# Output projection of a hybrid decoder step: tokens become the stationary operand, 512 weight columns stream past them

## The chip, the cores and the metric

One core of a Trainium2 chip runs the whole step in one launch. The metric is the device time of one execution in microseconds (us); a row of the profile gives times in us or, where it says so, in ns, counted from the first instruction of the profiled execution.

## What is computed

A decoder layer takes 512 prompt tokens and 8 x 4 sample tokens (544 in all, model width 2048) through an mLSTM branch and an attention branch. The change touches the last step alone: the merged branches `y`, times a 2048 x 2048 weight, plus a scaled residual, through a LayerNorm.

```python
def _layernorm(x, w, b):
    mu = jnp.mean(xf, axis=-1, keepdims=True)
    var = jnp.mean(jnp.square(xf - mu), axis=-1, keepdims=True)
    return (xf - mu) * lax.rsqrt(var + LN_EPS) * w + b
...
    y = (sigmoid(g_m) * einsum('btc,cd->btd', br_m, w_proj_m)
         + sigmoid(g_a) * einsum('btc,cd->btd', br_a, w_proj_a))
    out = jnp.einsum('btc,cd->btd', y, w_out)
    return _layernorm(DN_ALPHA * x + out, ln_w, ln_b)
```

All inputs and outputs are F32. Products keep F32 accuracy by a split: each operand is a rounded part (`wh`, `yh`, type F32R) and a rest (`wl`, `yl`), and three products `wh*yh`, `wh*yl`, `wl*yh` are summed in PSUM.

## The kernel before

The last stages are three runs over 16 tiles of 128 output columns each: the two branch projections (lines 1383 and 1399) and the output projection (line 1540). Each tile loads its weights from HBM as two halves of 8 k-tiles (`load_half`, line 182, the DMA of line 184 into one of three `raw` buffers of the pool `wr`), casts them on ScalarE (line 191, `wh`) and takes the rest on VectorE (line 192, `wl`), into two buffers of the pool `wp`; `products` (line 195, the matmul of line 200) then runs over k, the three products and two pieces of the token columns. The weights are stationary, the tokens move, and a result has its output column on the partition and its token along the bank.

The run at line 1399 makes `y`: VectorE multiplies the PSUM tile by a gate (line 1404), adds the other branch (line 1405), and `hilo` (lines 231 and 232) writes the parts `yh` and `yl`, 2048 x 544 each.

The output projection cuts the 544 tokens into 256 + 288 (`CUT`). Thirteen column tiles go through `gemm`; ScalarE copies the bank (`evac`, line 1463), TensorE transposes the copy back to tokens on partitions (line 1448 for the prompt, line 1455 for the 32 samples), and VectorE adds it to the residual `z` or `zs`, scaled by ALPHA (lines 1449, 1456). `zs` holds the samples as four quarters of 512 columns on four groups of 32 partitions. The last three column tiles multiply only the tokens from 256 on in that way. The other 256 tokens get those 384 columns from `rows_of` (line 1526, matmul of line 1536), in which the tokens are stationary and the weights move, while VectorE finishes the tiles that are complete: statistics (line 1461), `moments` (line 1474, with a power on GpSimd), and `finish` (line 1493), which takes 1280 columns in two passes on VectorE (lines 1505 and 1510) and 768 by VectorE, ScalarE and GpSimd (lines 1505, 1507, 1508), and stores.

The residual rows, the LayerNorm vectors and the samples' quarters of them come by DMAs of SyncE (`load_rows`, line 1423, `load_ln`, line 1431), in the same in-order queue as the weights. A scheduler sets the order of each engine's instructions; TensorE's is fixed by the code's own order only inside a `manual_schedule` block, which this stage does not use. PSUM has eight banks: four `sm` tiles (pool `psB`) and either two double-bank `mm` tiles or four `bank` tiles (`open_psum`, line 96).

Of the kernel before, what the change touches and what calls it, by code (L numbers as in the profile page):

```python
# [20 lines left out]
D = 2048  # L21
# [52 lines left out]
def _build(tc, nc, i, o, es):  # L74
# [1344 lines left out]
    wD = pool(esD, "wD", 1)  # L1419
# [8 lines left out]

    cq = d1.tile([128, 128], F32, name="cq")
# [10 lines left out]
    CUT = ((0, 0, 256), (1, 256, 288))  # L1440

    def add_residual(ct, ot, lo, hi):

        cs = slice(ct * 128, ct * 128 + 128)
        pt = sm()
        nb_ = min(hi, 4) - lo
        for t in range(lo, min(hi, 4)):
            PE.transpose(pt[:, (t - lo) * 128:(t - lo) * 128 + 128], ot[:, t * 128:t * 128 + 128], ident)  # L1448
        V.scalar_tensor_tensor(z[:, lo:lo + nb_, cs], z[:, lo:lo + nb_, cs], ALPHA, blk(pt[:, 0:nb_ * 128], nb_),
                               op0=ALU.mult, op1=ALU.add)  # L1450
        if hi == 5:
            q, c0 = ct // 4, (ct % 4) * 128
            r = slice(q * 32, q * 32 + 32)
            pt2 = sm()
            PE.transpose(pt2[:32, 0:128], ot[:, SEQ:T], ident)
            V.scalar_tensor_tensor(zs[r, c0:c0 + 128], zs[r, c0:c0 + 128], ALPHA, pt2[:32, 0:128],
                                   op0=ALU.mult, op1=ALU.add)

    def stats(lo, hi, c4):
        for t in range(lo, min(hi, 4)):  # L1460
            V.bn_stats(stt[:, t, c4], z[:, t, c4 * 512:c4 * 512 + 512])

    def evac(ot, ps, parts=(0, 1)):
        for f, c, w in CUT:
            if f in parts:
                A.copy(ot[:, c:c + w], ps[:, f, :w])

    def residual_task(ct, ot):
        add_residual(ct, ot, 0, 5)
        if ct % 4 == 3:  # L1470
            yield
            stats(0, 4, ct // 4)

    def moments(t):
        m = mv[:, t]
        if t < 4:
            V.bn_aggr(m[:, 0:2], stt[:, t])
            V.tensor_scalar(m[:, 1:2], m[:, 1:2], EPS, None, op0=ALU.add)
        else:
            V.bn_stats(stt[:, t, 0], zs)  # L1480
            V.bn_aggr(m[:, 0:2], stt[:, t, 0:1])
            V.scalar_tensor_tensor(m[:, 1:2], m[:, 0:1], m[:, 0:1], m[:, 1:2], op0=ALU.mult, op1=ALU.add)
            pm = sm()
            PE.matmul(pm[:, 0:2], cq[:], m[:, 0:2], start=True, stop=True)
            V.tensor_copy(m[:, 0:2], pm[:, 0:2])
            V.scalar_tensor_tensor(m[:, 3:4], m[:, 0:1], m[:, 0:1], m[:, 1:2], op0=ALU.mult, op1=ALU.subtract)
            V.tensor_scalar(m[:, 1:2], m[:, 3:4], -1.0, EPS, op0=ALU.mult, op1=ALU.add)
# [25 lines left out]
    def tail_task(ct, ot):  # L1513
        add_residual(ct, ot, 2, 5)
        yield

    def add_rows(t):

        cs = slice(D - G3 * 128, D)
        V.scalar_tensor_tensor(z[:, t, cs], z[:, t, cs], ALPHA, rows[t][:, 0:G3 * 128], op0=ALU.mult, op1=ALU.add)  # L1520
        stats(t, t + 1, 3)
        moments(t)

    rows = {}

    def rows_of(t, meanwhile):
        ps = rows[t] = sm()
        for k in range(KT):
            if k == 2:
                meanwhile()  # L1530
            yk = slice(t * 128, t * 128 + 128)
            hi, lo = yh_[k // 4][:, k % 4, yk], yl_[k // 4][:, k % 4, yk]
            for n, (a, p) in enumerate(((hi, 0), (hi, 1), (lo, 0))):
                for c, w, b in ((0, 256, w2[k // 8][p][:, k % 8].rearrange("p g c -> p (g c)")),
                                (256, 128, w1[k // 8][p][:, k % 8])):
                    PE.matmul(ps[:, c:c + w], a, b, start=(k == 0 and n == 0 and c == 0),
                              stop=(k == KT - 1 and n == 2 and c > 0), skip_group_check=True)

    G3 = 3
    for ct in range(16 - G3):  # L1540
        raws = [load_half(wo, ct * 128, half) for half in range(2)]
# [61 lines left out]
```

## Time and profile before

| | |
|---|---|
| median of 3 runs | 2565.08 us (2562.29 to 2566.04) |
| span of the profiled execution, first to last instruction | 2561.7 us |
| VectorE's last pass ends | 2557.7 us |
| TensorE's granted clock, mean over the span | 0.993 |
| ScalarE, GpSimd busy | 46%, 14% |
| instructions | 48818 |

The span is what the profile shows of one execution; the time of a run also holds what lies around it, and the profiled execution's own time is not given apart, so the median stands 3.4 us above this span and the fastest run 0.6. A row of an engine's timeline gives start, duration, engine, line, operation, output and input, shape and count, and in brackets how long the engine sat idle before it and what ended that. Matmuls overlap, so the distance between two starts, not the duration, tells what one costs.

### The profile page before, as it was taken

What the parts mean: (1) busy time and instruction counts of PE and PEld (TensorE: products, weight loads), DVE (VectorE), ACT (ScalarE), POOL (GpSimd) and SP (SyncE); (2) the same over time, 40 slices, a digit from 0 to 9 for tenths busy, and PEclk for the clock granted to TensorE, in tenths of its full rate; (3) what the DMA queues carried; (4) which work ended last, traced back from release to release, by engine and by line L of the source; (5) the groups of instructions that cost most, each with busy time, mean ns of one, the idle gap of its engine ahead of it and who ended that gap; (6) DMA issues with size and microseconds to landing.
All of it is one profiled execution on the core that took longest, in us unless ns stands there. A gap on an engine that the chain in (4) does not pass through costs nothing.

```text
span 2561.7 us, 48818 instructions
## 1 busy us (share of the span) xinstructions
PE 2524.2 (99%) x19994; PEld 2464.3 (96%) x19994; DVE 1707.2 (67%) x2508; ACT 1173.2 (46%) x1908; POOL 362.3 (14%) x334
## 2 busy tenths in 40 slices
PE   8999999999999999999999999999999999999997
PEld 8999999999999999899999998999999999999997
DVE  7867777777777777687777877777856553333236
ACT  4447667666666655333433433434633332222221
POOL 2111211211111111121121222221000000000002
PEclk9999999999999999999999999999999999999999
DMA  6566666666666663477576575676655455446332
GB/s 196 139 160 157 151 156 154 152 158 148 157 160 146 156 161 89 119 230 235 154 236 212 168 227 163 185 235 207 187 171 172 162 179 155 139 135 189 106 97 86
DMA packets 537103, 421.86 MB, mean 165 GB/s; under 512 B 43536, under 2 KB 449344, under 8 KB 536592
## 3 DMA queue, kind: packets, MB, share of 16 engines
q1 hardware_dynamic: 526800, 382.04, 49.8%
q0 software_dynamic: 10080, 36.70, 7.9%
q8 instruction: 157, 2.57, 0.4%
q14 instruction: 66, 0.54, 0.1%
HBM read 297.66 MB, written 86.42 MB: 150 GB/s over the span
## 4 chain that ended last, share of the span: by engine, by line
PE 57%; DVE 1%; issue 0%; POOL 0%; ACT 0%; DVEq 0%
PE mm L200 21%; PE bank L597 17%; PE bank L599 9%; PE sm L1266 2%; PE sm L1085 1%; PE sm L1079 1%; PE sm L1298 1%; PE sm L1311 1%; PE sm L200 1%; DVE z L1505 0%; PE sm L1245 0%; PE sm L1321 0%; PE sm L1253 0%; DVE z L1510 0%; PE sm L1448 0%
## 5 line engine op out<-in xcount | busy, mean ns | idle before, releaser
L191 ACT CAST wh<-raw 128x1024 fp32r<-128x1024 f32 x604 | 632.8, 1048 | 978.5 <-PE bank L597 599.3
L192 DVE TENSOR_TENSOR wl<-raw,wh 128x1024 fp32r<-128x1024 f32 x604 | 750.1, 1243 | 367.3 <-ACT wh L191 359.9
L597 PE MATMUL bank<-xk,wh 128*128 128x272 f32 x2304 | 312.7, 288 | 1.3 <-DVE ev L622 1.3
L597 PEld LDWEIGHTS bank<-xk,wh 128*128 128x128 f32 x2304 | 297.7, 188 | 4.2 <-ACT wh L191 2.4
L577 DVE TENSOR_TENSOR raw<-raw,raw 128x1024 f32<-128x1024 f32 x218 | 276.5, 1270 | 5.5 <-DMA raw<-in_w_in 2.9
L200 PE MATMUL mm<-bh,wl 128*128 128x272 f32 x1024 | 214.0, 289 | 0.0
L200 PE MATMUL mm<-bh,wh 128*128 128x272 f32 x1024 | 213.6, 290 | 0.0
L200 PE MATMUL mm<-bl,wh 128*128 128x272 f32 x1024 | 213.3, 288 | 0.0
L599 PE MATMUL bank<-xk,wl 128*128 128x272 f32 x1152 | 168.1, 288 | 0.0
L616 POOL TENSOR_TENSOR ev<-p,ev 128x272 f32<-128x272 f32 x72 | 105.0, 1458 | 424.9 <-ACT ev L615 404.4
L200 PEld LDWEIGHTS mm<-bh,wh 128*128 128x128 f32 x1024 | 160.7, 188 | 2.3 <-issue 2.3
L200 PEld LDWEIGHTS mm<-bl,wh 128*128 128x128 f32 x1024 | 161.4, 188 | 0.0
L200 PEld LDWEIGHTS mm<-bh,wl 128*128 128x128 f32 x1024 | 160.9, 189 | 0.0
L599 PEld LDWEIGHTS bank<-xk,wl 128*128 128x128 f32 x1152 | 153.4, 189 | 0.0
L597 PE MATMUL bank<-n2h,wh 128*128 128x272 f32 x576 | 149.1, 290 | 1.9 <-ACT wh L191 1.9
L597 PE MATMUL bank<-s1h,wh 128*128 128x272 f32 x576 | 150.5, 292 | 0.0
L597 PE MATMUL bank<-s1l,wh 128*128 128x272 f32 x576 | 149.3, 292 | 0.0
L597 PE MATMUL bank<-s4h,wh 128*128 128x272 f32 x576 | 149.0, 290 | 0.0
L597 PE MATMUL bank<-a11h,wh 128*128 128x272 f32 x576 | 148.7, 290 | 0.0
L597 PE MATMUL bank<-n2l,wh 128*128 128x272 f32 x576 | 148.7, 291 | 0.0
L597 PE MATMUL bank<-a11l,wh 128*128 128x272 f32 x576 | 148.5, 291 | 0.0
L597 PE MATMUL bank<-n3l,wh 128*128 128x272 f32 x576 | 148.2, 290 | 0.0
(427 smaller groups left out, 5489.7 us busy)
## 6 DMA issues: line engine op xcount, KB each, us to landing
raw<-in_w_in SPq DMA_DIRECT2D x296, 512.0 KB, 4.4
raw<-raw POOLq DMA_DIRECT2D x70, 512.0 KB, 4.9
C<-in_state_mlstm_C SPq DMA_DIRECT2D x32, 1024.0 KB, 5.6
out<-C SPq DMA_DIRECT2D x64, 512.0 KB, 3.8
raw<-in_w_proj_a SPq DMA_DIRECT2D x32, 512.0 KB, 5.6
raw<-in_w_proj_m SPq DMA_DIRECT2D x32, 512.0 KB, 4.3
raw<-in_w_out SPq DMA_DIRECT2D x32, 512.0 KB, 4.3
d_sgm<-ev SPq DMA_DIRECT2D x16, 272.0 KB, 3.9
```

What stands on the lines that cost most here:

```text
L191: A.copy(wh[:], raw[:])
L192: V.tensor_tensor(out=wl[:], in0=raw[:], in1=r32(wh[:]), op=ALU.subtract)
L200: PE.matmul(ps[:, f, :w], a[:, kk], b(k, c, w), start=(k == 0 and n == 0), stop=(k == 15 and n == 2))
L577: V.tensor_tensor(out=w[out][:], in0=w[a][:], in1=w[b][:], op=ALU.add)
L597: PE.matmul(ps, wh[:, k], x(p, k), start=(first and k == 0 and p == 0), stop=False, skip_group_check=True)
L599: PE.matmul(ps, wl[:, k], x(0, k), start=False, stop=(k == 7), skip_group_check=True)
L616: G.tensor_tensor(out=c22, in0=p1, in1=c11, op=ALU.subtract)
L1079: PE.matmul(pC[c * 32:c * 32 + 32, :], qz[:, c], ct[:, c], start=(b == 0), stop=(b == NB - 1), tile_position=(0, c * 32))
L1085: PE.matmul(pu[:], Ab[:, c * 128:c * 128 + 128], r["V4"][:], start=True, stop=True)
L1266: PE.matmul(pp[:, 0:258], a[:, b * 128:b * 128 + 128], b_[:, b, f], start=(b == 0 and n == 0), stop=(b == 3 and n == 2))
L1298: PE.matmul(pp[:, 0:n], x_[c][:, b * 128:b * 128 + 128], y_[c][:, b * 128:SEQ], start=(c == 0 and m == 0), stop=(c == 3 and m == 2))
L1311: PE.matmul(pp[:, 0:258], x_[:, off:off + 128], y_[:, b, f], start=(b == 0 and n == 0), stop=(b == j and n == 2))
```

## The change

`y` becomes the stationary operand for the whole projection. Four blocks of 512 output columns are computed; in each, four banks hold the four tiles of 128 prompt tokens (`ps`), one more the samples (`acc`). Weights come in chunks of two k-tiles by 512 columns (`wide`), eight to a block; six chunks have buffers for their parts (two in `wp`, four in `wD`), three for their raw form. A result already has its token on the partition, so VectorE adds the residual straight from the bank (`add_rows`). The 32 sample tokens are no longer columns of the matmuls above: a copy `ysf` in F32 is the stationary operand of 32-column matmuls on four column groups, one k-tile each, against the raw F32 weights (`samples_by`); one more matmul with a selection matrix sums the four groups (`add_samples`). TensorE's order is fixed by the code (`manual_schedule`). In blocks 0 to 2 the tiles share each pair of chunks; in block 3 they share the first four chunks, then the samples take the last four, then the tiles are completed one by one, each followed by its LayerNorm.

```diff
+    ysf = pool(es, "ysp", 1, side="left").tile([128, KT, NS], F32, name="ysf")
...
         hilo(sg[:], yh_[ct // 4][:, ct % 4], yl_[ct // 4][:, ct % 4])
+        A.copy(ysf[:, ct], sg[:, SEQ:T])
...
-    wD = pool(esD, "wD", 1)
+    wD = pool(esD, "wD", 4)
...
+    def wide(cb, j):
+        raw = wr.tile([128, 2, 512], F32, tag="raw", name=nm("raw"))
+        nc.sync.dma_start(raw[:], wo[:, 2 * j:2 * j + 2, cb * 512:cb * 512 + 512])
+        p = wp if j % 6 < 2 else wD
+        wh, wl = (p.tile([128, 2, 512], F32R, tag=t_, name=nm(t_)) for t_ in ("wh", "wl"))
+        hilo(raw[:], wh[:], wl[:])
+        return wh, wl, raw
+
+    def rows_by(ps, t, ks, chunks):
+        yk = slice(t * 128, t * 128 + 128)
+        for k in ks:
+            wh, wl = (w[:, k % 2] for w in chunks[k // 2][:2])
             hi, lo = yh_[k // 4][:, k % 4, yk], yl_[k // 4][:, k % 4, yk]
+            for n, (a, b) in enumerate(((hi, wh), (hi, wl), (lo, wh))):
+                PE.matmul(ps[:], a, b, start=(k == 0 and n == 0), stop=(k == KT - 1 and n == 2))
+
+    def samples_by(ps, ks, chunks):
+        for k in ks:
+            g = k % 4
+            PE.matmul(ps[g * 32:g * 32 + 32, :], ysf[:, k], chunks[k // 2][2][:, k % 2], start=(k < 4), stop=(k >= KT - 4),
+                      tile_position=(0, g * 32))
+
+    def add_rows(t, cb, ps):
+        cs = slice(cb * 512, cb * 512 + 512)
+        V.scalar_tensor_tensor(z[:, t, cs], z[:, t, cs], ALPHA, ps[:], op0=ALU.mult, op1=ALU.add)
+        V.bn_stats(stt[:, t, cb], z[:, t, cs])
+
+    def add_samples(cb, sq, ps):
+        q = slice(cb * 32, cb * 32 + 32)
+        PE.matmul(ps[q, :], cc[:, C_SEL:C_SEL + 32], sq[:], start=True, stop=True, tile_position=(0, cb * 32))
+        V.scalar_tensor_tensor(zs[q], zs[q], ALPHA, ps[q, :], op0=ALU.mult, op1=ALU.add)
...
+    with tc.manual_schedule(engines={PE.engine}):
+        open_psum(True)
+        for cb in range(4):
+            mine, other = (sm, bank) if cb % 2 == 0 else (bank, sm)
+            chunks = {}
+            if cb == 0:
+                chunks.update({j: wide(cb, j) for j in range(2)})
+                for q in range(4):
+                    load_rows(q)
+            ps = [mine() for _ in range(4)]
+            acc = other()
+            last = cb == 3
+            for j in range(0, 4 if last else 8, 2):
+                for jj in (j, j + 1):
+                    if jj not in chunks:
+                        chunks[jj] = wide(cb, jj)
+                samples_by(acc, range(2 * j, 2 * j + 4), chunks)
+                for ks in ((2 * j, 2 * j + 1), (2 * j + 2, 2 * j + 3)) if last or j < 6 else (range(12, 16),):
+                    for t in range(4):
+                        rows_by(ps[t], t, ks, chunks)
+                        if not last and j == 6:
+                            add_rows(t, cb, ps[t])
+            if cb == 1:
+                load_ln()
+            if not last:
+                sq = ev(512)
+                A.copy(sq[:], acc[:])
+                add_samples(cb, sq, other())
+        for j in (4, 6):
+            for jj in (j, j + 1):
+                chunks[jj] = wide(cb, jj)
+            samples_by(acc, range(2 * j, 2 * j + 4), chunks)
+        sq = ev(512)
+        A.copy(sq[:], acc[:])
+        for t in range(4):
+            rows_by(ps[t], t, range(8, 12), chunks)
...
+            rows_by(ps[t], t, range(12, 16), chunks)
+            add_rows(t, 3, ps[t])
+            moments(t)
+            scale_of(t)
+            finish(t, LAST if t == 3 else CHUNKS)
```

At the first dots of the last loop tile 0 runs `add_samples` and the samples' statistics, tile 1 their normalisation and stores. `finish` keeps its passes, chunk by chunk.

Three places show how the built order moves. The first is SyncE's queue at the start of the output projection. Before, `raw_27165` is the sixth weight load of the stage (the second half of column tile 2), and the eight quarter loads follow `lb`:

```order
L1432 DMA cq<-in_consts 128x128
L1433 DMA lw<-in_ln_w 128x2048
L184 DMA raw_27165<-in_w_out 128x8x128
L1434 DMA lb<-in_ln_b 128x2048
L1437 DMA zs_26920<-in_ln_w 32x512
```

Now, with `raw_27101` the sixth weight load (chunk 5 of block 0, k-tiles 10 and 11) and the pair of quarter loads standing four times:

```order
L1433 DMA cq<-in_consts 128x128
L1434 DMA lw<-in_ln_w 128x2048
L1435 DMA lb<-in_ln_b 128x2048
L1438 DMA zs_26940<-in_ln_w 32x512
L1439 DMA zs_26941<-in_ln_b 32x512
...
L1478 DMA raw_27101<-in_w_out 128x2x512
L1478 DMA raw_27159<-in_w_out 128x2x512
```

Five weight loads stand ahead of `z` in both; the sixth has moved behind `lb` and all quarters, and the vectors that the code asks for after block 1 stand in block 0.

The second place is TensorE's queue in block 3, where the tiles' first halves end and their second halves begin. `raw_27928`, `raw_27934`, `raw_27944` and `raw_27950` are chunks 4 to 7, `sm_27799` the samples' accumulator, `bank_27798` and `bank_27795` tiles 3 and 0:

```order
L1491 MATMUL bank_27798<-wh_27872,yl_25036 128x512
L1497 MATMUL sm_27799<-raw_27928,ysf 32x512 x2
L1497 MATMUL sm_27799<-raw_27934,ysf 32x512 x2
L1497 MATMUL sm_27799<-raw_27944,ysf 32x512 x2
L1497 MATMUL sm_27799<-raw_27950,ysf 32x512 x2
L1491 MATMUL bank_27795<-wh_27930,yh_25033 128x512
L1491 MATMUL bank_27795<-wl_27931,yh_25033 128x512
```

Nothing like it stood there before: the samples were columns of each tile's matmuls. All four raw chunks are now read in one run, and nothing else of TensorE's lies between.

The third place is VectorE's queue at the end. Before, where the prompt tiles `z` finish (`sm_28731` and `sm_28872` are the two banks of `rows_of`):

```order
L1510 SCALAR_TENSOR_TENSOR z<-z,mv,lb 128x1280
L1520 SCALAR_TENSOR_TENSOR z<-z,sm_28731 128x384
L1486 SCALAR_TENSOR_TENSOR mv<-mv 128x1
L1496 SCALAR_TENSOR_TENSOR zs_26919<-zs_26919,mv,zs_26920 128x512
L1461 BN_STATS stt<-z 128x6
```

Now, with `bank_27797` and `bank_27798` the banks of tiles 2 and 3:

```order
L1460 SCALAR_TENSOR_TENSOR z<-z,mv,lw 128x1280
L1505 SCALAR_TENSOR_TENSOR z<-z,bank_27797 128x512
L1465 SCALAR_TENSOR_TENSOR z<-z,mv,lb 128x1280
L1506 BN_STATS stt<-z 128x6
L1443 BN_AGGR mv<-stt 128x2
L1445 TENSOR_SCALAR mv<-mv 128x1
L1460 SCALAR_TENSOR_TENSOR z<-z,mv,lw 128x768
L1460 SCALAR_TENSOR_TENSOR z<-z,mv,lw 128x1280
L1505 SCALAR_TENSOR_TENSOR z<-z,bank_27798 128x512
```

The add and the statistics of each tile now stand between the passes of the tile ahead of it, for all four tiles; before, two tiles went through this end and two had been finished ahead.

## Rows read from the trace of the kernel before

**Rows 1.** The page, whole span: busy time of the engines and the chain that ended last

```profile
PE 2524.2 (99%) x19994; PEld 2464.3 (96%) x19994; DVE 1707.2 (67%) x2508; ACT 1173.2 (46%) x1908; POOL 362.3 (14%) x334
...
PE 57%; DVE 1%; issue 0%; POOL 0%; ACT 0%; DVEq 0%
```

**Rows 2.** Timeline of TensorE, start and end of the output projection

```profile
2341.96 0.41 PE L200 MATMUL mm<-yh,wh 128*128 128x256 f32 x2
2342.21 0.41 PE L200 MATMUL mm<-yl,wh 128*128 128x256 f32 x2
...
2547.09 0.22 PE L1536 MATMUL sm<-wh,yl 128*128 128x128 f32 x1
```

**Rows 3.** Timeline of TensorE in the sample phase, 1169 to 1176

```profile
1169.51 1.16 PE L599 MATMUL bank<-s4h,wl 128*128 128x272 f32 x8
1170.60 1.07 PE L1079 MATMUL sm<-C,qz 128*32 128x512 f32 x8
1171.59 0.72 PE L1085 MATMUL sm<-V,Ab 128*128 128x512 f32 x2
1172.15 2.17 PE L597 MATMUL bank<-xk,wh 128*128 128x272 f32 x16
1174.16 1.17 PE L599 MATMUL bank<-xk,wl 128*128 128x272 f32 x8
1175.16 0.62 PE L1085 MATMUL sm<-V,Ab 128*128 128x512 f32 x2
1175.62 0.29 PE L597 MATMUL bank<-a11h,wh 128*128 128x272 f32 x1
```

**Rows 4.** Timeline of VectorE where the output projection starts

```profile
2342.16 0.72 DVE L1404 TENSOR_TENSOR c<-mm,c 128x544 f32<-128x544 f32 x1 [3.91 <-PE mm L200]
...
2343.56 1.22 DVE L192 TENSOR_TENSOR wl<-raw,wh 128x1024 fp32r<-128x1024 f32 x1
```

**Rows 5.** Timeline of SyncE's queue, 2340 to 2380 (start and time of the issue)

```profile
2345.28 0.52 SPq L1426 DMA_DIRECT2D z<-in_x_prompt  x1
...
2356.43 5.51 SPq L1434 DMA_DIRECT2D lb<-in_ln_b  x1
...
2370.96 0.31 SPq L1438 DMA_DIRECT2D zs<-in_ln_b  x1
2371.37 7.14 SPq L184 DMA_DIRECT2D raw<-in_w_out  x4
```

**Rows 6.** Waits of SyncE's queue, 2340 to 2380: total, times, longest

```profile
SPq L1438 <- DMA lb<-in_ln_b: 3.7, 1, 3.7
```

**Rows 7.** Timeline of ScalarE, and from the page the DMA issues (KB, landing)

```profile
2375.81 1.05 ACT L191 CAST wh<-raw 128x1024 fp32r<-128x1024 f32 x1 [7.14 <-DMA raw<-in_w_out]
...
raw<-in_w_out SPq DMA_DIRECT2D x32, 512.0 KB, 4.3
```

**Rows 8.** Timeline of TensorE, then windows (busy by engine, clock, DMA share, GB/s)

```profile
42.54 0.59 PE L200 MATMUL mm<-a11h,wh 128*128 128x272 f32 x1 [2.38 <-ACT ev L529]
...
42.50:43.00 0.50, 0.46 (x2) 0.46 (x3) 0.50 (x2) 0.45 (x4) 0.00 (x0) 0.50 0.61 155
...
45.50:46.00 0.50, 0.50 (x5) 0.50 (x5) 0.50 (x3) 0.00 (x0) 0.50 (x2) 0.87 0.51 125
```

**Rows 9.** Timeline of VectorE, the last 18 us

```profile
2544.14 2.47 DVE L1505 SCALAR_TENSOR_TENSOR z<-z,mv,lw 128x768 f32<-128x768 f32 x2
2546.53 0.74 DVE L1497 SCALAR_TENSOR_TENSOR zs<-zs,mv,zs 128x512 f32<-128x512 f32 x1
2547.19 3.09 DVE L1510 SCALAR_TENSOR_TENSOR z<-z,mv,lb 128x1280 f32<-128x1280 f32 x1
2550.20 0.54 DVE L1520 SCALAR_TENSOR_TENSOR z<-z,sm 128x384 f32<-128x384 f32 x1
...
2551.87 3.47 DVE L1505 SCALAR_TENSOR_TENSOR z<-z,mv,lw 128x384 f32<-128x384 f32 x4
2555.26 2.40 DVE L1510 SCALAR_TENSOR_TENSOR z<-z,mv,lb 128x896 f32<-128x896 f32 x2
```

More of the change, by code (lines that the diff above doesn't have):

```diff
@@ L1418, in _build @@
     mv = d1.tile([128, 5, 4], F32, name="mv")
-    wD = pool(esD, "wD", 1)
+    cq = d1.tile([128, 128], F32, name="cq")
+    wD = pool(esD, "wD", 4)
     ys_rows = y_s.rearrange("b t d -> (b t) d")
@@ L1438, in load_ln, with moments, scale_of @@
             nc.sync.dma_start(lbq[r], i["ln_b"][cs].partition_broadcast(32))
[L1440 to L1474, printed above, removed]
+    def moments(t, n=4):
         m = mv[:, t]
+        V.bn_aggr(m[:, 0:2], stt[:, t, 0:n])
         if t < 4:
-            V.bn_aggr(m[:, 0:2], stt[:, t])
             V.tensor_scalar(m[:, 1:2], m[:, 1:2], EPS, None, op0=ALU.add)
[L1479 to L1487, printed above, removed]
+    def scale_of(t):
+        m = mv[:, t]
         G.tensor_tensor(out=m[:, 2:3], in0=m[:, 1:2], in1=mh[:, 0:1], op=ALU.pow)
@@ L1511, in finish @@
             nc.sync.dma_start(dst[:, c], zt)
[L1513 to L1531, printed above, removed]
-            hi, lo = yh_[k // 4][:, k % 4, yk], yl_[k // 4][:, k % 4, yk]
[L1533 to L1537, printed above, removed]
@@ L1539, in _build @@
-    G3 = 3
-    for ct in range(16 - G3):
-        raws = [load_half(wo, ct * 128, half) for half in range(2)]
-        if ct % 3 == 0 and ct < 12:
-            load_rows(ct // 3)
-        elif ct == 10:
-            load_ln()
-        ps = gemm(wo, ct * 128, yh, yl, cols=CUT, raws=raws)
-        ot = ev()
-        evac(ot, ps)
-        spawn(residual_task(ct, ot))
-    w2 = [[wD.tile([128, 8, 2, 128], F32R, name=nm("w2")) for p in range(2)] for half in range(2)]
-    w1 = []
-    for g in range(G3):
-        ct = 16 - G3 + g
-        ps = sm()
-        for half in range(2):
-            raw = load_half(wo, ct * 128, half)
-            if g < 2:
-                wh, wl = (w[:, :, g] for w in w2[half])
-                hilo(raw[:], wh, wl)
-            else:
-                w1.append(split(raw))
-                wh, wl = w1[half]
-            products(ps[:].unsqueeze(1), half, wh, wl, yh, yl, ((0, 256, 288),))
-        ot = ev()
-        A.copy(ot[:, 256:T], ps[:, 0:288])
-        if g < G3 - 1:
-            spawn(tail_task(ct, ot))
@@ L1569, in _build, with finish_samples @@
-    rows_of(0, lambda: (add_residual(15, ot, 2, 5), stats(2, 4, 3), [moments(t) for t in (2, 3, 4)], finish(2), finish(3), finish(4)))
-    rows_of(1, lambda: (add_rows(0), finish(0)))
-    add_rows(1)
-    finish(1, LAST)
-    drain()
+    def finish_samples():
+        m, r_ = mv[:, 4, 0:1], mv[:, 4, 2:3]
+        V.scalar_tensor_tensor(zs, zs, m, lwq, op0=ALU.subtract, op1=ALU.mult)
+        V.scalar_tensor_tensor(zs, zs, r_, lbq, op0=ALU.mult, op1=ALU.add)
+        for q in range(4):
+            nc.sync.dma_start(ys_rows[:, q * 512:q * 512 + 512], zs[q * 32:q * 32 + 32])
```

29 lines of the change are left out of this document (22 added, 7 removed).

## The prediction

> **What bounds the kernel now.** I read the page first: TensorE is busy for 99% of the span, VectorE for two thirds, and the chain that ended last is mostly TensorE with a short VectorE end [rows 1]. So a change in this stage is worth what it does to TensorE's queue, plus what it does to the end, where TensorE has finished and VectorE has not. I then read TensorE's own timeline of the stage. The output projection's first matmul starts at 2341.96 and its last ends at 2547.3, 205.3 us later, with a weight-stationary pair (256 + 288 columns) every 0.25 us [rows 2]. That is 544 columns at 2.4 GHz (226.7 ns) and about 12 ns per matmul. From 2547.3 to the span's end at 2561.7 another 14.4 us pass in VectorE's LayerNorm and the last stores [rows 9]. Last I read SyncE's queue at the stage's start, since the residual rows, the LayerNorm vectors and the weights all go through it [rows 5, 6].
>
> **The matmuls.** The change has 4 blocks of 512 columns x 4 token tiles x 16 k x 3 products = 768 matmuls of 512 columns; the 1,584 shorter ones and all residual transposes go. No 512-column stream of this length is in the trace, so I bound one matmul. Below: a 272-column matmul follows the next by 0.125 us (eight from 1174.16 to 1175.16), and 240 more columns at 2.4 GHz add 0.100, so 0.225. Above: the two 512-column matmuls at 1175.16 give way at 1175.62, 0.230 each [rows 3]. I take 0.228, nearer to the row of the same width: 768 x 0.228 = 175.1 us (ends 172.8 and 176.6).
>
> **The sample tokens.** They leave the moving side and become 32-column F32 stationaries, four k's side by side on four column groups, 16 such groups. The trace has this very shape: four F32 matmuls of 32 x 512 on four column groups. The eight 272-column matmuls that start at 1169.51 would give way at 1170.51; the group starts at 1170.60, takes 0.99, and the two 512-column matmuls behind it take 0.56 where they take 0.46 without it [rows 3]. So 0.09 + 0.99 + 0.10 = 1.18 us a group, with both switches of mode in it: 16 x 1.18 = 18.9 us (low end 16 x 0.99). Each block ends with one F32 matmul that adds the four groups; a single one can cost no more than four, so 4 x 0.99 = 4.0 us as the upper end, which I take.
>
> TensorE's sum: 175.1 + 18.9 + 4.0 = 198.0 us against 205.3, **7.3 us less**.
>
> **The start.** The change opens another PSUM pool, and its first matmul (the sample accumulator, first in TensorE's fixed order) waits for VectorE to read the last tile of the old one. That read starts at 2342.16 and takes 0.72 [rows 4]; with 0.07 for the hand-over TensorE starts at 2342.95, 1.0 us late. The casts and splits of the first two weight chunks go beside it.
>
> **The end.** Before, two token tiles are finished while TensorE still works; now all four get their last columns in the last 23 us. Call T0 the start of the first tile's second half: TensorE needs 96 x 0.228 + 1.0 = 22.9 us from there. The first tile's sum is ready at T0 + 24 x 0.228 + 1.0 = 6.5, VectorE starts at 6.7 and from there has no gap. A tile costs it 1.8 (add, statistics, mean: from 2550.20 to 2551.87 in the trace, and 0.15 more for the wider add), 2.4 (weight pass, 2544.14 to 2546.53) and 3.0 (bias pass beside GpSimd), 7.2 together. Three tiles are 21.6, the samples' normalisation in between two passes of 0.74 and small ones, 2.0. The last tile's smaller pieces take 1.8 + 3.4 + 2.4 = 7.6, and from VectorE's end (2555.26 + 2.40 = 2557.66) to the span's end 4.0 us remain [rows 9]. That is T0 + 41.9, or 19.0 us behind TensorE instead of 14.4: **4.6 us more**. Up to here 1.0 - 7.3 + 4.6 = -1.7 us.
>
> **The first stall: weights behind the residual rows.** The raw F32 weights are now read by TensorE itself, for the samples, so each of the three raw buffers is held until TensorE gets there, and samples of k 8 to 11 need raw chunks 4 and 5 both. SyncE's built order puts chunk 5 behind all of z, lw, lb and the eight quarter vectors (the source asks for the last three in the second block only; the order hoists them). Before, one weight load stood between lw and lb. Each DMA there waits for one eight places ahead of it: the last quarter waited 3.7 us for lb to land [rows 6], left at 2370.96, and the next weight load at 2371.37 [rows 5]; its cast began at 2375.81, ended by that DMA [rows 7]. The rows from z on start at the same moment as before (2345.28): two weight loads now go out ahead, one when the first sample matmuls have read raw chunk 0 (about 2343.9), one when VectorE has split chunk 1, third in its queue as the split of 2343.56 was before, which ended at 2344.8 [rows 4]. About the same bytes lie ahead of lb, half a megabyte earlier in place of the one in the middle. So chunk 5 lands at about 2375.8. TensorE wants it at 2342.95 + 1.18 + 10.94 (48 x 0.228) + 1.18 + 10.94 + 0.6 = 2367.8. **Stall 8.0 us**; ends 4 (a queue that drains faster without the load in the middle) and 10. The cast and split of chunk 5 then hide under chunk 4's 24 matmuls; chunk 7 only needs buffer 4's, read before the stall, and its place in the queue.
>
> **The second stall: four raw chunks, three buffers.** In the last block the samples of k 8 to 15 stand in one run, ahead of the tiles' second halves. Chunk 7 goes into chunk 4's buffer, which that same run frees. With the run's start as zero, the first quarter's results are out at 0.95, the load goes at 1.0 and lands 4.3 later [rows 7], at 5.3; TensorE is there at 1.77. **Stall 3.5 us**; ends 2.5 (larger pieces land faster) and 4.5.
>
> **The clock.** After 2.38 us without work TensorE restarted at 42.54 at the low level: 0.50 in the slice from 42.5, and it rose in the slice from 45.5 to 46 [rows 8]. Some 3.1 us at 1.2 instead of 2.4 GHz cost 1.5 us. Both stalls are longer than 2.38 us: 2 x 1.5 = 3.0 us (ends 0 and 3.4).
>
> Elsewhere a pair of chunks lasts TensorE 10.9 us, and the later load of a pair lands 4.3 after its buffer is free, the cast and split 2.3 after that: hidden by 4 us [rows 4, 7]. At a block's end the next chunk's buffers come free 1.4 us ahead, and the F32 matmul and the first sample group (2 us) cover its cast and split. The sixteen small sample copies cost nothing: ScalarE waits for others before its casts there [rows 7]; were that cover gone, sixteen times well under the 1.05 of a cast thirty-two times as wide.
>
> **The sum**: -1.7 + 8.0 + 3.5 + 3.0 = +12.8 us on the span's 2561.7, 2574.5. The shown runs' median, 2565.08, lies 3.4 above that span, which I keep: **2577.9 us**.
>
> **The rivals.**
> *Not slower, because the weights are not late.* For: with DMA at its best SyncE could reach chunk 5 earlier; if it lands by 2367.8 (issued by 2363.5, not 2371.4) the first stall and its clock go, which gives 2577.9 - 9.5 = 2568.4. If chunk 7 were also in time, another 5.0 go: 2563.4, no change. Against: the wait for lb is in the trace, and three buffers cannot hold four chunks. 0.08 for the first alone, 0.04 for both.
> *Much faster, because 512-column matmuls overlap.* If a stream of them cost far less than its columns, TensorE's sum would fall. The rows speak against it: two at 0.230 each. Were one to take no longer than a 272-column one, 0.125, that is 768 x 0.103 = 79 us less, some 2499 us, and more stalls, since a pair of chunks would last 6 us. Chance 0.01. The Trainium skill's TensorE: Matmul & The Clock Gate, section Back-to-back issue gap, states about 131 ns a matmul at N=512 in sustained load-and-multiply streams; by this rule the 768 would take an estimated 100.6 us where the rows give 175.1, and the trace does not agree.
> *Much slower, because the column groups take turns.* If the four F32 matmuls of a group ran one after the other, 16 x 3 x 0.99 = 47.5 us more, 2625. Against: the same shape took 0.99 for all four [rows 3]. 0.02.
>
> **Chances.** The forecast keeps 0.85. A measurement of this kernel tells about 0.2%, 5.1 us, from no change. Faster by more: 0.03 (0.01 for overlap, the rest from low ends with no stall). Within: 0.13 (half of the first-stall-hidden case, most of the case with neither, and 0.05 of the forecast, with all low ends). Slower: 0.84. With the low ends (172.8, 4, 2.5, no clock) the time is 2567 to 2568; with the high ones (176.6, 10, 4.5, 3.4, and 2 to 4 us for groups and end) 2587. Range 2568 to 2588.
>
> **What would show it.** Right: 512-column matmuls 0.225 to 0.230 apart; sample groups of 1.1 to 1.2; TensorE idle 7 to 9 us, some 25 us into the stage, ended by a raw weight DMA, and again 3 to 4 us ahead of the last block's second halves, each with a clock of 0.50 behind it; VectorE alone for the last 19 us. Wrong: no gap there, or gaps of that size at every pair of chunks, which would mean that loads are late everywhere.

## The result, and the profile after

The changed kernel takes 2578.68 us (median of 5 runs, 2575.11 to 2584.6) against 2565.08 (2562.29 to 2568.26, 5 runs): a ratio of 1.0047, 95% interval 1.003 to 1.0064. (Here and below the ratio is estimated from all executions of both kernels, so it need not equal the quotient of the two medians.) Forecast were 2577.9 us and slower. The profiled run is the slowest of the five, 2584.6 us with a span of 2582.8.

The profiles of this kernel and of its variants reach the output projection at different times, 2342.0 to 2348.3 us after the start, although TensorE's work ahead of the stage is the same: the granted clock between 1020 and 1080 us was anything from 0.86 to 0.94. So I compare the **stage**: from the end of TensorE's last matmul of the branch projection (before, the start of the next one; now 0.25 us after the start of its last row of two) to the end of the span. Before it ran from 2341.96 [rows 2] to 2561.7, 219.7 us. Now it runs from 2348.03 to 2582.8, 234.8 us: **15.0 us more**, where 12.8 were forecast.

The page of the changed kernel (span; busy time by engine; the chain that ended last) shows little, as in [rows 1]:

```profile
span 2582.8 us, 47283 instructions
...
PE 2529.0 (98%) x19240; PEld 2411.2 (93%) x19240; DVE 1704.5 (66%) x2494; ACT 1168.9 (45%) x1899; POOL 359.3 (14%) x334
...
PE 55%; DVE 1%; DMA 1%; issue 0%; POOL 0%; ACT 0%; SPq 0%; DVEq 0%
```

The chain now has a DMA in it. TensorE's timeline of the stage in the changed kernel answers to [rows 2, 3]; a sample group of four F32 matmuls is counted as x8, half a group as x4:

```profile
2347.78 0.41 PE L200 MATMUL mm<-bh,wl 128*128 128x272 f32 x2
2349.01 1.06 PE L1497 MATMUL bank<-raw,ysf 128*32 128x512 f32 x8 [0.82 <-DVE c L1405]
...
2373.70 1.05 PE L1497 MATMUL bank<-raw,ysf 128*32 128x512 f32 x4
2381.97 1.92 PE L1497 MATMUL bank<-raw,ysf 128*32 128x512 f32 x4 [7.22 <-DMA raw<-in_w_out]
2383.82 0.80 PE L1491 MATMUL sm<-wh,yh 128*128 128x512 f32 x1
2384.41 0.63 PE L1491 MATMUL sm<-wl,yh 128*128 128x512 f32 x1
...
2396.34 1.06 PE L1497 MATMUL bank<-raw,ysf 128*32 128x512 f32 x8
...
2446.20 0.40 PE L1491 MATMUL bank<-wh,yl 128*128 128x512 f32 x1
2446.53 1.06 PE L1497 MATMUL sm<-raw,ysf 128*32 128x512 f32 x8
2447.53 0.50 PE L1491 MATMUL bank<-wh,yh 128*128 128x512 f32 x1
...
2458.55 0.39 PE L1491 MATMUL bank<-wh,yl 128*128 128x512 f32 x1
2458.88 0.62 PE L1511 MATMUL sm<-ev,cc 128*32 128x512 f32 x1
...
2460.71 0.50 PE L1491 MATMUL sm<-wh,yh 128*128 128x512 f32 x1
...
2534.60 1.91 PE L1497 MATMUL sm<-raw,ysf 128*32 128x512 f32 x12
2539.47 1.40 PE L1497 MATMUL sm<-raw,ysf 128*32 128x512 f32 x4 [2.96 <-DMA raw<-in_w_out]
...
2544.98 1.04 PE L1511 MATMUL sm<-ev,cc 128*32 128x512 f32 x2
...
2565.64 0.39 PE L1491 MATMUL bank<-wh,yl 128*128 128x512 f32 x1
```

TensorE stands idle three times: 0.82 us at the start, 7.22 us in the first block and 2.96 us in the last, the latter two ended by a raw weight DMA. Behind the 7.22 us the matmuls start 0.43 apart (2384.41 and the four rows behind it), which is the low clock: the windows below show 0.50 there. SyncE's queue shows why, as in [rows 5], and ScalarE's cast the landing, as in [rows 7]:

```profile
2351.38 0.41 SPq L1429 DMA_DIRECT2D z<-in_x_prompt  x1
...
2363.93 0.33 SPq L1435 DMA_DIRECT2D lb<-in_ln_b  x1
...
2377.48 0.31 SPq L1439 DMA_DIRECT2D zs<-in_ln_b  x1
2377.89 20.44 SPq L1478 DMA_DIRECT2D raw<-in_w_out  x6
```

```profile
2381.94 1.04 ACT L231 CAST wh<-raw 128x1024 fp32r<-128x1024 f32 x1 [23.59 <-DMA raw<-in_w_out]
```

Chunk 5's load leaves 26.5 us after the first residual rows, as before (2371.37 - 2345.28 = 26.1), and it lands at 2381.94; the forecast, moved by the 6.07 us by which this stage starts later, was 2381.9. The windows of TensorE (busy time by engine, clock, DMA share, GB/s) show the clock falling within the first wait, and at the second only at about 2540.0, 0.5 us behind the restart:

```profile
2376.00:2378.00 2.00, 0.00 (x0) 0.00 (x0) 0.00 (x0) 0.00 (x0) 0.00 (x0) 1.00 0.13 42
...
2380.00:2382.00 2.00, 0.03 (x2) 0.04 (x4) 0.00 (x0) 0.06 (x1) 0.00 (x0) 0.50 0.93 303
...
2384.00:2386.00 2.00, 2.00 (x5) 1.62 (x6) 1.47 (x2) 1.74 (x2) 0.00 (x0) 0.50 0.20 69
2386.00:2388.00 2.00, 2.00 (x9) 1.58 (x9) 1.23 (x1) 0.00 (x0) 0.00 (x0) 0.89 0.59 204
...
2538.00:2540.00 2.00, 0.53 (x4) 0.14 (x4) 0.00 (x0) 0.48 (x1) 0.00 (x0) 1.00 0.35 133
2540.00:2542.00 2.00, 2.00 (x7) 1.02 (x4) 1.23 (x1) 1.15 (x2) 0.00 (x0) 0.51 0.00 0
```

At the end VectorE sets the pace, as in [rows 9]: of the last 34 us nearly 30 are its work and 4.0 the last stores. Its first add there and its last pass are

```profile
2549.06 0.69 DVE L1505 SCALAR_TENSOR_TENSOR z<-z,bank 128x512 f32<-128x512 f32 x1 [1.10 <-PE bank L1491]
...
2576.36 2.40 DVE L1465 SCALAR_TENSOR_TENSOR z<-z,mv,lb 128x896 f32<-128x896 f32 x2
```

From TensorE's end (2566.0) to the span's end 16.8 us pass; before, 14.4.

### The profile page after: what moved, and what is told of

Its sections match the earlier page's. It is cut to its first block, busy times and chain, and to the rows that moved or that the text cites. A ratio compares the mean times of both kernels' runs of the same rounds, so it can differ in the third digit from the quotient of the medians.

```text
span 2582.8 us, 47283 instructions
## 1 busy us (share of the span) xinstructions
PE 2529.0 (98%) x19240; PEld 2411.2 (93%) x19240; DVE 1704.5 (66%) x2494; ACT 1168.9 (45%) x1899; POOL 359.3 (14%) x334
## 3 DMA queue, kind: packets, MB, share of 16 engines
q8 instruction: 151, 2.47, 0.4%
## 4 chain that ended last, share of the span: by engine, by line
PE 55%; DVE 1%; DMA 1%; issue 0%; POOL 0%; ACT 0%; SPq 0%; DVEq 0%
PE bank L597 17%; PE mm L200 15%; PE bank L599 8%; PE bank L1491 3%; PE sm L1491 3%; PE sm L1266 2%; PE sm L1085 1%; PE sm L1079 1%; PE sm L1298 1%; PE sm L1311 1%; DMA lb<-in_ln_b 1%; DMA z<-in_x_prompt 0%; DVE z L1465 0%; DVE z L1460 0%; PE sm L1497 0%; DMA raw<-in_w_out 0%
## 5 line engine op out<-in xcount | busy, mean ns | idle before, releaser
L191 ACT CAST wh<-raw 128x1024 fp32r<-128x1024 f32 x576 | 603.4, 1048 | 856.1 <-PE bank L597 603.0
L192 DVE TENSOR_TENSOR wl<-raw,wh 128x1024 fp32r<-128x1024 f32 x576 | 715.5, 1243 | 309.2 <-ACT wh L191 302.1
L200 PE MATMUL mm<-bl,wh 128*128 128x272 f32 x1024 | 213.3, 288 | 0.0
L597 PE MATMUL bank<-n3h,wh 128*128 128x272 f32 x576 | 148.9, 290 | 0.0
```

The costliest lines, as they stand in the source:

```text
L191: A.copy(wh[:], raw[:])
L192: V.tensor_tensor(out=wl[:], in0=raw[:], in1=r32(wh[:]), op=ALU.subtract)
L200: PE.matmul(ps[:, f, :w], a[:, kk], b(k, c, w), start=(k == 0 and n == 0), stop=(k == 15 and n == 2))
L597: PE.matmul(ps, wh[:, k], x(p, k), start=(first and k == 0 and p == 0), stop=False, skip_group_check=True)
```

## The experiments

The theory is the prediction's: the first wait comes from the LayerNorm vectors ahead of chunk 5 in SyncE's queue, the second from four raw chunks in three buffers, and each costs clock as well. Each run's total is given with its ratio to the kernel before, which ran beside it on the same chip (its medians: 2564.1 us beside runs 1 to 4, 2567.2 beside 5 to 8, 2565.3 beside 9 to 11), and the stage of its one profiled execution:

| kernel | median us (runs) | ratio, 95% interval | stage us |
|---|---|---|---|
| before | 2565.08 (5) | | 219.7 |
| changed | 2578.68 (5) | 1.0047, 1.003 to 1.0064 | 234.8 |
| 1 vectors later | 2570.34 (11) | 1.002, 1.001 to 1.003 | 224.7 |
| 2 last block's samples divided | 2578.32 (6) | 1.0046, 1.0033 to 1.006 | 230.2 |
| 3 both | 2568.02 (12) | 1.0008, 0.9999 to 1.0018 | 220.5 |
| 4 a fourth buffer | 2577.53 (4) | 1.0044, 1.003 to 1.0059 | 231.8 |
| 5 changed, again | 2581.13 (6) | 1.0052, 1.0036 to 1.0068 | 233.9 |
| 6 work in the first wait | 2578.38 (7) | 1.0041, 1.0026 to 1.0055 | 233.8 |
| 7 a quarter of the samples | 2554.54 (4) | 0.9951, 0.9933 to 0.9969 | 206.0 |
| 8 tiles finished earlier | 2560.97 (11) | 0.9979, 0.9968 to 0.9989 | 214.9 |
| 9 as 8, no GpSimd | 2558.72 (6) | 0.9974, 0.9962 to 0.9986 | 213.3 |
| 10 as 8, pools exchanged | 2561.96 (11) | 0.9983, 0.9972 to 0.9994 | 213.7 |
| 11 as 8, both | 2556.63 (5) | 0.9966, 0.9954 to 0.9979 | 212.1 |

An interval of 0.2 to 0.35% is 5 to 9 us wide, so most steps below are read from the stage and its rows, and the totals only bear them out where they are large.

### 1. The vectors later

```diff
-            if cb == 1:
-                load_ln()
...
+        load = nc.sync.dma_start(raw[:], wo[:, 2 * j:2 * j + 2, cb * 512:cb * 512 + 512])
+        if cb in (1, 2) and ln:
+            with tc.issue_after(load.ins):
+                nc.sync.dma_start(*ln.pop(0))
```

`ln` is the list of `cq`, `lw`, `lb` and the eight quarters; `issue_after` puts a DMA behind another in the queue.

> The eleven LayerNorm vector loads leave SyncE's queue ahead of weight chunk 5 and go out one by one, each behind a weight load of the second and third block. Stage = from the first TensorE row of the output projection's turn (the start of the old last tile's end) to the span's end: 234.8 us in the changed kernel, 219.7 in the kernel before. Theory (the vectors stand ahead of chunk 5 in the queue): the wait of 7.2 us on the raw weights some 25 us into the stage goes, and with it the slow clock and split group behind it, 2.4: stage 224.6, total about 2568.5. Rival (TensorE holds the raw buffers too long, so chunk 5 could not be loaded sooner, or the residual rows alone delay it): the wait stays at 4 to 8 us, stage 230 to 235, total 2574 to 2579.

The wait in the first block is gone and the stage is 224.7 us, 10.1 less, as the theory said; the total fell to 2570.3, where about 2568.5 was expected. TensorE's timeline of this kernel has the third sample group in one piece, and the second wait stays:

```profile
2367.80 1.06 PE L1497 MATMUL bank<-raw,ysf 128*32 128x512 f32 x8
...
2523.49 1.59 PE L1497 MATMUL sm<-raw,ysf 128*32 128x512 f32 x4 [2.91 <-DMA raw<-in_w_out]
```

So without the vectors ahead of it chunk 5 is not late: the samples' hold on the raw buffers and the residual rows alone do not suffice. That the hold is needed too, run 7 shows.

### 2. The last block's samples divided

```diff
+        samples_by(acc, range(8, 12), chunks)
...
         for t in range(4):
             rows_by(ps[t], t, range(8, 12), chunks)
             if t == 0:
+                samples_by(acc, range(12, 16), chunks)
+                sq = ev(512)
+                A.copy(sq[:], acc[:])
+            elif t == 1:
                 add_samples(3, sq, other())
```

> Last block: the samples of k 12 to 15 are taken after the first token tile's k 8 to 11 in place of directly behind the samples of k 8 to 11, so 12 matmuls (2.8 us) stand between the buffer's release and the chunk that needs it. Theory (four raw chunks in three buffers): the second wait shrinks from 3.0 to under 1 us and the slow clock behind it goes, together 4 to 5.4 us: stage 229.4 to 231, total 2573 to 2575. Rival (the load is late for another reason, the queue or VectorE's split): the wait moves but stays about 3 us, total 2578 to 2579. The first wait is unchanged in both.

The stage met the theory (230.2), with 12 matmuls in the gap; the last two sample groups on TensorE's timeline:

```profile
2534.48 1.07 PE L1497 MATMUL sm<-raw,ysf 128*32 128x512 f32 x8
...
2538.45 1.80 PE L1497 MATMUL sm<-raw,ysf 128*32 128x512 f32 x8
```

The second takes 0.7 us longer than a whole group at once, since its raw weights come only just in time; the clock stays at 1.00 behind it. The total did not meet it: 2578.3 where 2573 to 2575 were expected. An interval of 7 us cannot show 4, and the first wait and the start of the stage differ by about as much from run to run, so the total alone would have decided nothing.

### 3. Both

> Both edits together. Theory: the two costs are independent and add up, stage 219.5 to 221, total 2564 to 2566, level with the kernel before (2565.1): what is left is 3 us fewer on TensorE and 4.6 us more at VectorE's end. Rival (TensorE then runs into loads that are late elsewhere, or the slow clock comes back for another reason): total 2570 or more.

The stage is 220.5 us, within 0.8 of the kernel before, and 14.3 less than the changed kernel's; the two edits alone gave 10.1 and 4.6, so they add up. The total is 2568.0 where 2564 to 2566 were expected: 0.08% above before, with an interval that includes no change, and this profile's stage starts 4.7 us later than before's. Chunk 5's cast and the group that needs it, on ScalarE and TensorE of this kernel, stand 2.4 us apart (2369.91 is chunk 5's cast here):

```profile
2369.91 1.05 ACT L231 CAST wh<-raw 128x1024 fp32r<-128x1024 f32 x1 [14.00 <-DMA raw<-in_w_out]
```

```profile
2372.31 1.06 PE L1497 MATMUL bank<-raw,ysf 128*32 128x512 f32 x8
```

### 4. A fourth raw buffer, for one chunk

```diff
+    wx = pool(esD, "wx", 1)
...
-        raw = wr.tile([128, 2, 512], F32, tag="raw", name=nm("raw"))
+        raw = (wx if (cb, j) == (3, 7) else wr).tile([128, 2, 512], F32, tag="raw", name=nm("raw"))
```

> One raw weight buffer more, used by chunk 7 of the last block alone; nothing else changes. Theory (three buffers for four chunks make the second wait): the second wait goes wholly, with the clock and split group behind it, 5.4 us: stage 229.4, total about 2573.3; the first wait stays at 7 to 8. Rival (SyncE's queue or DMA makes the load late): the wait stays at about 3 us and the total at 2578.7.

The second wait is gone: on TensorE's timeline both groups run as one row, and only the first block's wait is left, this time 9.04 us long.

```profile
2378.26 1.92 PE L1498 MATMUL bank<-raw,ysf 128*32 128x512 f32 x4 [9.04 <-DMA raw<-in_w_out]
...
2531.61 1.93 PE L1498 MATMUL sm<-raw,ysf 128*32 128x512 f32 x16
...
2536.45 1.05 PE L1512 MATMUL sm<-ev,cc 128*32 128x512 f32 x2
```

From the first group's start to the matmul that adds the four groups it is 4.84 us; in the changed kernel 10.38 (2534.60 to 2544.98). So the second wait cost 5.5 us in all. The stage is 231.8, not 229.4, because the first wait was 1.8 us longer than in the first profile and the clock cost more behind it. The total, 2577.5 where about 2573.3 was expected, again moved by less than its interval. So the 5.5 us rest on the rows of single executions: the totals of runs 2 and 4 fell by 0.4 and 1.2 us, and that of run 3 lies 2.3 below run 1's, less than the stages say each time, though within the intervals.

### 5. The changed kernel again

> The changed kernel once more, beside the next three. Stage (first TensorE row of the output projection's turn to span's end) was 234.8 us in its first profile and the total 2578.7; in the runs with the second wait taken away the total fell by only 0.4 to 1.2 us, where the profiled stages were 3 to 4.5 shorter. Theory: the first wait varies from run to run (6.6 to 9.0 us seen), so this profile shows a stage of 232 to 235 and the total is 2577 to 2580. Rival: the first profile was an outlier, stage 230 or less, total 2574 to 2576, and the second wait is then worth less than the 5.4 us read from it.

The stage is 233.9, as the theory allowed, and the total 2581.1, 1.1 us above its range, so the first profile was no outlier. The first wait was 5.68 us; over the four profiles that have it as in the changed kernel it was 5.7, 6.6, 7.2 and 9.0.

### 6. Work in the first wait

```diff
+                if (cb, j) == (0, 4):
+                    samples_by(acc, range(8, 10), chunks)
+                    pf = bank()
+                    for n in range(30):
+                        PE.matmul(pf[:], yh_[0][:, 0, 0:128], chunks[3][0][:, 0], start=True, stop=True)
+                    samples_by(acc, range(10, 12), chunks)
```

> Thirty extra matmuls of 128 x 512 (7.0 us, into an otherwise unused PSUM tile) stand between the two halves of the sample group that waits in the first block, so TensorE has work during most of the first wait. They add nothing to the output. Theory (an idle TensorE loses its clock, 1.2 GHz for some us after the wait): the granted clock stays at 1.0 through the stretch, and from the landing of the raw weights (the end of the wait) to the end of the 48 matmuls behind it TensorE needs 1.5 to 2.4 us less than in the changed kernel; stage 232.4 to 233.3, total 1.5 to 2.4 below the changed kernel. Rival (the slow matmuls behind the wait come from the weights' cast and split, not from the clock): that stretch is as long as before.

TensorE's timeline of this kernel:

```profile
2373.96 1.05 PE L1497 MATMUL bank<-raw,ysf 128*32 128x512 f32 x4
2374.94 7.10 PE L1548 MATMUL bank<-wh,yh 128*128 128x512 f32 x30
2381.97 1.05 PE L1497 MATMUL bank<-raw,ysf 128*32 128x512 f32 x4
...
2394.27 1.06 PE L1497 MATMUL bank<-raw,ysf 128*32 128x512 f32 x8
...
2537.38 1.92 PE L1497 MATMUL sm<-raw,ysf 128*32 128x512 f32 x4 [2.94 <-DMA raw<-in_w_out]
```

The second half of the group starts at 2381.97 as in the changed kernel, and the next group comes 12.30 us later, there 14.37 (2381.97 to 2396.34): with the clock kept (1.00 in every window from 2374 to 2396), 2.07 us are saved, as the theory said. Each half of a group takes 0.98 to the next instruction, as long as a whole one: a wait between the halves costs a second 0.98. The stage missed its range: 233.8 is 1.0 shorter than in the changed kernel's first profile and level with its second. The second wait cost more clock here. It was as long (2.94), but the low clock came earlier, before the half group began, and lasted longer:

```profile
2536.00:2538.00 2.00, 0.62 (x2) 0.19 (x4) 0.00 (x0) 0.56 (x1) 0.00 (x0) 0.72 0.30 114
...
2542.00:2544.00 2.00, 2.00 (x7) 1.50 (x5) 0.00 (x0) 0.00 (x0) 0.00 (x0) 0.57 0.00 0
```

From the half group to the adding matmul (2544.25 here) it is 6.87 us, in the changed kernel 5.51 and with full clock 0.98 + 2.99 = 3.97 (2.99 from the first of the 12 matmuls in run 4, at 2533.46): the same wait cost 1.5 us of clock there and 2.9 here. The total, 2578.4, is 0.3 us below the changed kernel's first median and 2.8 below its second, so it decides nothing.

### 7. A quarter of the samples

```diff
         for k in ks:
+            if k >= 4:
+                continue
             g = k % 4
-            PE.matmul(ps[g * 32:g * 32 + 32, :], ysf[:, k], chunks[k // 2][2][:, k % 2], start=(k < 4), stop=(k >= KT - 4),
+            PE.matmul(ps[g * 32:g * 32 + 32, :], ysf[:, k], chunks[k // 2][2][:, k % 2], start=True, stop=True,
```

> The sample groups of k 4 to 15 are left out, so the sample output is computed from a quarter of its sum; the other 12 groups' TensorE time and their hold on the raw weight buffers go. Weight chunk 5 then stands ahead of the residual rows in SyncE's queue and chunk 6 and 7 ahead of the vectors. Theory (groups cost 1.2 us each, both waits come from the samples' reading the raw weights): no wait over 1 us, stage 220.5 (the version without waits) minus 12 x 1.2 = 206.1, total about 2551. Rival (the group's time is hidden or the waits have another cause): stage 210 or more.

The stage is 206.0 us, the theory's 206.1; the total is 2554.5 where about 2551 was expected. No wait on a raw DMA is left; one of 0.89 us on VectorE's split is. So 12 groups cost about 14.5 us (220.5 - 206.0), 1.2 each, all of it on the path; the two kernels also differ in the vectors' place and in the last block's order, which this takes to cost nothing.

The first wait is gone here although the vectors still go out in the first block: in SyncE's queue chunk 5's load is now the last of three issued from 2345.40 on, ahead of the first residual rows at 2347.72. So the first wait needs both: the samples' hold, which puts chunk 5 behind rows and vectors, and the vectors.

### 8. Tiles finished earlier

With the vectors later and the samples divided, what was left against the kernel before was VectorE's end. In the last block k 0 to 3 go first for all tiles, and then each tile its k 4 to 15:

```diff
-            for j in range(0, 4 if last else 8, 2):
+            for j in range(0, 2 if last else 8, 2):
...
         for t in range(4):
-            rows_by(ps[t], t, range(8, 12), chunks)
+            rows_by(ps[t], t, range(4, 12), chunks)
```

The sample groups of k 4 to 11 stand ahead of the tiles' turns, that of k 12 to 15 in tile 0's.

> The vector loads moved as in the first run, and the last block divided otherwise: k 0 to 3 for all four token tiles, then k 4 to 15 tile by tile (36 matmuls, 8.4 us a tile, longer than VectorE's 7.2 for finishing one), samples of k 4 to 15 in three groups between. Theory: the waits stay away and VectorE ends 12 us behind TensorE in place of 19 (last add, statistics, the last tile's passes, 4 us of stores): stage 220.5 - 7 = 213.5, total 2558 to 2560, 5 us faster than the kernel before. Rival (six chunks in 25 us are more than three raw buffers and one queue can bring): a wait of 2 to 6 us ahead of the samples of k 8 to 15 and the slow clock behind it, stage 216 to 222, total 2561 to 2568.

TensorE's last matmul in run 3:

```profile
2550.07 0.39 PE L1491 MATMUL bank<-wh,yl 128*128 128x512 f32 x1
```

TensorE's last matmul and two of VectorE's rows in this kernel:

```profile
2544.52 0.40 PE L1491 MATMUL bank<-wh,yl 128*128 128x512 f32 x1
```

```profile
2518.52 0.69 DVE L1505 SCALAR_TENSOR_TENSOR z<-z,bank 128x512 f32<-128x512 f32 x1 [3.69 <-PE bank L1491]
...
2532.44 3.08 DVE L1462 SCALAR_TENSOR_TENSOR z<-z,mv,lb 128x1280 f32<-128x1280 f32 x1
```

No raw weights are late, and the span ends 12.0 us behind TensorE (2544.92 to 2556.9), as expected. The stage is 214.9, 5.6 less than in run 3 and not 7: the end behind TensorE had been 16.6 us in run 3 (2550.46 to 2567.1) and not the forecast's 19, so 12.0 is only 4.6 less; the other 0.9 is less time on TensorE. VectorE has hardly a gap from 2518.52 on: the two tiles with the samples' work cost it 9.5 and 9.9 us, more than TensorE's 8.4 a tile. The total is 2561.0 where 2558 to 2560 were expected, faster than the kernel before by 0.21% (0.11 to 0.32).

### 9 to 11. GpSimd's share, and the start

```diff
-    CHUNKS = ((1280, 2048, True), (0, 1280, False))
-    LAST = ((1280, 1664, True), (1664, 2048, True), (0, 896, False), (896, 1280, False))
+    CHUNKS = ((1024, 2048, False), (0, 1024, False))
+    LAST = ((0, 1024, False), (1024, 1664, False), (1664, 2048, False))
```

> The version with early tiles, with GpSimd's share of the bias pass given back to VectorE (two halves of 1024 columns, the last tile in pieces of 1024, 640 and 384), ScalarE's scaling with it. There VectorE works without a gap over the last 34 us, and its bias pass of 1280 columns takes 3.08 us beside GpSimd's add of 768, where a weight pass over 1280 columns takes 1.54. Theory (the two engines slow each other, so the 768 columns given to GpSimd save VectorE nothing): a tile's bias pass over all 2048 columns takes about 2.5 us, 0.6 less on each of three tiles and about 0.5 on the last, stage 214.9 - 2 = 212.9, total about 1.5 to 2.3 below the version with early tiles. Rival (VectorE's bias pass is slow by itself): 2048 columns take 4.9, stage 220 or more.

A tile's bias pass on VectorE is now

```profile
2524.11 2.47 DVE L1462 SCALAR_TENSOR_TENSOR z<-z,mv,lb 128x1024 f32<-128x1024 f32 x2
```

2048 columns take 2.47 us where 1280 beside GpSimd's add took 3.08. The stage is 213.3, 1.6 less (2.0 expected); the ratio is 0.9974 against run 8's 0.9979, which alone would not tell them apart. VectorE now waits for TensorE's tiles again (1.39, 0.83 and 1.13 us).

The edit also takes ScalarE's scaling away. The trace of the kernel before shows that GpSimd is what matters: there the same pass over 1280 columns also runs once with GpSimd and ScalarE idle, and takes 1.54 us; the one that starts at 2547.19 [rows 9] takes 3.09 beside GpSimd's add:

```profile
2540.34 1.54 DVE L1510 SCALAR_TENSOR_TENSOR z<-z,mv,lb 128x1280 f32<-128x1280 f32 x1
```

```profile
2546.60 2.33 POOL L1508 TENSOR_TENSOR z<-z,lb 128x768 f32<-128x768 f32 x1 [1.05 <-ACT z L1507]
```

That add ends at 2548.93 and the pass 1.35 us later; in all 32 such passes of these traces the pass ends 1.34 to 1.36 us after GpSimd's add, so it gets hardly anywhere while the add runs. ScalarE's scaling is over before each of them starts. This agrees with the Trainium skill, SBUF — State Buffer, section SBUF: two separate sides, by which a VectorE instruction with two inputs in SBUF and a GpSimd instruction that reads SBUF take turns on a shared pair of ports.

```diff
-            mine, other = (sm, bank) if cb % 2 == 0 else (bank, sm)
+            mine, other = (bank, sm) if cb % 2 == 0 else (sm, bank)
```

> The version with early tiles, with the two PSUM pools' roles exchanged block by block, so that the first sample group adds up in a pool that is already open. Theory (the 0.82 us wait and 0.98 late start come from the newly opened pool, whose space VectorE still reads): the first group starts without a wait, directly behind the last matmul of the stage before, and the token tiles that now need the new pool come 1.2 us later, when VectorE has read it: stage 214.9 - 1.0 = 213.9. Rival (the first group waits for the new tokens or the raw weights): the wait stays at 0.8 us, stage 214.9.

TensorE goes from the old stage to the first sample group without a wait:

```profile
2347.77 0.41 PE L200 MATMUL mm<-bh,wl 128*128 128x272 f32 x2
2348.11 1.07 PE L1497 MATMUL sm<-raw,ysf 128*32 128x512 f32 x8
```

and the stage is 213.7, 1.2 less than in run 8; the new pool was the cause. The total, 2562.0 with a ratio of 0.9983, shows nothing of it: from one execution to another the stage's start alone differs by up to 6.0 us, as between this profile and that of run 8.

> Both edits of the last two together. Theory: stage 214.9 - 3 = 211.9, total 3 us below the version with early tiles and 8 to 9 below the kernel before, which it beats by 0.3%. Rival (VectorE, which ends the span, starts its last 34 us no earlier although TensorE does): only the 2 us of the first edit remain.

Both together: a stage of 212.1, and 2556.6 us, faster than the kernel before by 0.34% (0.21 to 0.46). This version beats both kernels.

## Why the prediction was right

The forecast, its sign and the places of the lost time held, and runs 1, 2, 4 and 7 bear out both causes. Against the stage of before (205.3 on TensorE, 14.4 behind it), term by term, from the first profile of the changed kernel:

| term | forecast us | measured us |
|---|---|---|
| 768 matmuls | 175.1 | 178.4 |
| 16 sample groups | 18.9 | 19.2 |
| 4 matmuls that add the groups | 4.0 | 3.7 |
| start | 1.0 | 0.98 |
| first wait, with the group it divides | 8.0 | 8.2 |
| clock behind it | 1.5 | 2.1 |
| second wait, with the group it divides | 3.5 | 4.0 |
| clock behind it | 1.5 | 1.5 |
| behind TensorE | 19.0 | 16.8 |
| sum, against 219.7 | +12.8 | 234.9, +15.2 |

The sum meets the measured 234.8 within 0.1 us; smaller pieces, such as the two last groups side by side and the small matmul of line 1522, cancel in it. That the total came within 0.8 us of the forecast is partly luck: the stage is 2.2 us off it, the matmuls' 3.3 too little is in part made up by 2.2 too much at the end, and the changed kernel's own median moved by 2.5 us between the two times it was run. The 3.4 us that the forecast kept between span and median was partly chance too: a run's time lies 1.8 above its span (2584.6 and 2582.8), so the profile of before came from a run 1.6 us faster than its median.

- **The matmuls.** 48 starts, from the one at 2447.53 to one at 2458.55, are 0.232 us apart (11.02 us less 0.10 for the switch back from the samples, over 47 intervals): 768 take 178.4 us, beyond the upper end of 176.6. This term lies outside its bounds, and so does the clock: 3.6 us for both waits against at most 3.4. The bound from above came from two matmuls between narrower ones [rows 3]; a long run is 1% dearer. Why was not tested. At 0.232 a piece the rival that 512-column matmuls overlap is out.
- **The sample groups.** 1.00 us, and 0.10 of switching on either side (2446.20, 2446.53 and 2447.53 above), 1.20 against 1.18; run 7 gives 1.2 from the whole stage. The column groups do not take turns.
- **The adding matmuls** were taken at their upper end; from 2458.88 to 2460.71 one with the group behind it takes 1.83, so 0.83 beside the group's 1.00, and the last, alone, 0.98 and a switch on either side, 1.2.
- **The first wait.** Its cause is shown by runs 1 and 7. Its end was forecast within 0.1 us; TensorE fell idle at 2374.75, 0.9 later than forecast (2367.8 moved by 6.07), half of it for the dearer matmuls and half because half a group took 0.98 and not 0.6. Of the 22.64 us from 2373.70 to 2396.34 an undisturbed group and its 48 matmuls take 12.34 (2522.26 to 2534.60); 10.3 are lost: 7.22 of waiting, 2.07 of clock (run 6) and 1.0 because the group is run as two halves, for which the forecast added nothing: it took each half at half the price.
- **The second wait.** Its cause is shown by runs 2 and 4, 5.5 us in all in the traced executions: 2.96 of waiting where 3.5 was forecast, 1.0 for the divided group and 1.5 of clock.
- **The clock** was priced from one restart [rows 8] at 1.5 us. Behind the second wait it cost 1.5 to 1.6 in three profiles and 2.9 in one; behind the first 2.1 to 2.8 in four (14.37 to 15.08 us from the half group to the next group, 12.30 with the clock kept).
- **The end.** From the start of the tiles' second halves (2540.79) to the span's end it is 42.0 us, against 41.9 in the forecast. VectorE started 1.6 us later than forecast, behind the low clock, and made it up, mostly with bias passes of 2.6 to 2.7 in place of 3.0. TensorE took 25.2 us from there and not 22.9, which shortens what is left behind it to 16.8.

What the change itself promised, fewer matmul columns on TensorE, came to 205.3 - (178.4 + 19.2 + 3.7) = 4.0 us, not 7.3, and VectorE's end and the start take 3.4 of it back. The two waits, about 15.8 us with all they bring, did the rest; with both taken away (run 3) the kernels stand level within the interval.

## What to carry to other kernels

When an operand that only VectorE and ScalarE read is now read by TensorE as well, its buffers are held until TensorE's turn: count the buffers against every run of instructions that needs several of them at once, and look at what stands ahead of the next load in its in-order queue. A wait of TensorE is dearer than its length (here 7.2 and 3.0 us became 10.3 and 5.5), through the clock and through a group of small matmuls that no longer runs side by side. And where several finished tiles leave a serial end on another engine, finish tiles at that engine's pace: dividing the last block otherwise gained 5.6 us, more than the 4.0 that the change itself took off TensorE.

## What was not expected of the hardware

- Half of a four-group sample step takes as long as the whole: 0.98 us for two matmuls on two column groups as for four on four (run 6).
- The same idle time of 2.9 to 3.0 us cost 1.5 us of clock in one run and 2.9 in another (runs 5 and 6): in the first the granted clock fell behind the restart, in the second before it. What decides that was not tested.
- VectorE's bias pass over 1280 columns beside GpSimd's add of 768 took 2.4 to 3.1 us, always ending 1.34 to 1.36 after the add; without GpSimd 1280 columns take 1.54 and all 2048 take 2.47. GpSimd's help cost more than it saved.
